# Pairs of heads in a two-layer trunk: bias and x loads behind the weights, two modulation chunks into the output projection, one bias tile a pair

## The chip, the core and the metric

One core of a Trainium2 chip runs the whole kernel. The metric is the device time of one execution in microseconds (us), as the median of three runs. Beside it stands one execution taken by the profiler, from which all durations below come. TensorE (PE) multiplies; VectorE (DVE), ScalarE (ACT) and GpSimd (POOL) work on tiles; all loads of weights, biases and modulation chunks are issued by SyncE (SP), in the order of its queue.

## The reference

A trunk of two layers on x of 256 tokens by 1024 features, in float32. Layer 0 mixes tokens by dilated sliding-window attention, layer 1 by gated linear attention; a gated ConvFFN follows each. Each sub-layer's input is normalised and shifted, scaled and gated by terms worked out from a conditioning vector c. The change lies in layer 0's attention:

```python
qkv = (h @ w_in).reshape(B, S, A_GROUPS, 3, A_HEADS, A_HEAD_DIM)   # 3 dilations, 16 heads of 64
for g, (window, dilation) in enumerate(A_CONFIGS):
    o, lse = dilated_branch(q[g] * scale, k[g], v[g], rel_bias[g], window, dilation)
...
s = einsum(qb, kk) + bias          # bias depends on the distance and the head alone
p = exp(s - max(s)); o = p @ vv / sum(p)
...
o = sum(softmax(lse over g) * o_g) @ w_out
```

## The kernel before

**Products.** Every float32 product is made of three on TensorE: with a weight split into a high part `whi` and a remainder `wlo`, and the input into `hhi` and `hlo`, `mm3` (L172) adds hi by hi, hi by lo and lo by hi. `split` (L155) loads a weight into a `raw` buffer (L159), ScalarE casts it to `whi` in two halves (L165), VectorE subtracts to get `wlo` in two halves (L169). There are four `raw` buffers and three pairs of `whi` and `wlo`. A `raw` buffer is free again when its `wlo` is made.

**Modulation.** The terms from c come in 48 chunks of 1 MB. `ada_chunk` (L129) loads one into a `raw` buffer of the same four (L133), VectorE makes two dot products with c (L138, names `ada_raw` and `dot`), ScalarE adds the constants. `next_ada` takes the next chunk of the list; a chunk can be taken anywhere before its terms are wanted.

**Heads in pairs.** The 16 heads go in eight pairs u = 0 to 7. The first stage (0 to 59 us) loads 8 chunks and the weight `w0`, which holds queries and keys of pairs 0 and 1 and the values of pair 0. Then, for the pairs that follow:

- `queries(u, g)` for the three dilations g = 0, 1, 2: weight `wqk` of 1 MB, products into the bank `pqk`, evacuation to `q` (ScalarE) and `k` (VectorE, L492; for g = 0 both parts by L494 to L499), and one `next_ada`;
- `values(u, half)`: two weights `wv` of 768 KB, products into two banks `pv`, one for each half of the tokens. These two banks and those of `pqk` share two buffers of PSUM (tag `p`): a bank can be written again only when its evacuation is done;
- `scores`, `probabilities` (VectorE adds the bias and takes the maximum, ScalarE makes the exponential, VectorE scales), `turn` (transposes `t` on TensorE, copied to `pt` by ScalarE and VectorE in turns), `outputs` (bank `po`, split into `ohi` and `olo`);
- `by_group` copies the two banks `pv` into tiles `v` (L506 to L509), where the tokens stand in order of residue.

`outputs(u - 1)` runs between scores of pair u and its probabilities. After pair 7 comes `project` with the weight `w_out_a`, in which the last pair's transposes and outputs are placed between products.

**Biases.** The bias of a head depends on the distance alone and lies in DRAM as a row (`rows_d`). `load_bias(u)` reads a pair's two rows shifted by partition: for each head and each half of the partitions one load of 64 x 258 (L347) and one of 64 x 2 x 64 (L348), so 8 loads a pair, of 64.5 and 32 KB. `bias_of` places them behind the last weight load that was written.

**Order.** The order on each engine is made by the framework's scheduler from the order in which the code is written and from the hints `behind` and `tc.issue_after`, which put an instruction after another in the scheduler's reckoning. Each engine then runs its list strictly in order. SyncE's DMAs take turns on eight semaphores, so a DMA is issued only when the one eight issues earlier has landed.

The functions and their line numbers in the profile:

Of the kernel before, what the change touches and what calls it, by code (L numbers as in the profile page):

```python
# [11 lines left out]
F32 = mybir.dt.float32  # L12
# [6 lines left out]
P = 128  # L19
D = 1024  # L20
T = 256
# [7 lines left out]
CH = 64  # L29
# [6 lines left out]
NROW = 768  # L36
KEYS = T + 2 * CH
# [20 lines left out]
def trunk(ctx: ExitStack, tc: tile.TileContext, I, out):  # L58
    nc = tc.nc
# [26 lines left out]
    x_all = state.tile([P, KT, T], F32, name="x_all")  # L86
# [158 lines left out]
    @contextmanager  # L245
    def behind(*those):

        with ExitStack() as st:
            for i in those:
                st.enter_context(tc.issue_after(i.ins))  # L250
            yield
# [85 lines left out]
    def load_bias(u):  # L337

        r, both = rows_d[:, :], []
        for hh in range(2):
            b = att.tile([P, KEYS + 2], F32, tag=f"bias{hh}", name="bias")
            at = r.offset + (2 * u + hh) * NROW
            for odd in range(2):
                own = slice(CH * odd, CH * odd + CH)
                nc.sync.dma_start(b[own, 2 * CH :], bass.AP(r.tensor, at + odd, [[4, CH], [1, T + 2]]))  # L347
                nc.sync.dma_start(b[own, 0 : 2 * CH].rearrange("p (g x) -> p g x", g=2),  # L348
                                  bass.AP(r.tensor, at + 512, [[1, CH], [P, 2], [1, CH]]))
            both.append(b[:, :])  # L350
        return both


    sq = wspl.tile([P, 2048], F32, tag="wlo", name="sq").rearrange("p (k t) -> p k t", k=KT)
# [39 lines left out]
        if kt == 1:  # L394
            scale_terms(1)
    with tc.issue_after(last_load[0].ins):
        nc.sync.dma_start(x_all, I["xT"])
        nc.sync.dma_start(rows_d, rows)
        nc.sync.dma_start(small[:, C_CW:], I["small"][:, C_CW:])

# [3 lines left out]
    def next_ada():  # L404
        if rest:
            ada_chunk(*rest.pop(0))
# [94 lines left out]
    def by_group(v, pv, n):  # L501


        copy = (nc.scalar.copy, nc.vector.tensor_copy)[n]
        top, low = slice(0, CH), slice(CH, P)
        copy(v[top, 0 : 2 * P], pv[top, 0 : 2 * P])  # L506
        copy(v[low, :].rearrange("p (g x) -> p g x", g=3)[:, ::2, :], pv[low, 0 : 3 * P].rearrange("p (g x) -> p g x", g=3)[:, ::2, :])
        nc.scalar.copy(v[low, P : 2 * P], pv[top, 2 * P : 3 * P])
        nc.scalar.copy(v[top, 2 * P : 3 * P], pv[low, P : 2 * P])  # L509

    def new_qk():
        q = [[att.tile([P, T], F32R, tag=f"q0{i}", name="q") for i in range(2)]]
# [39 lines left out]
    def bias_of(u):  # L552
        with tc.issue_after(last_load[0].ins):
            return load_bias(u)
# [14 lines left out]
        for i in range(2 * NG):  # L569
            mm3(pqk1[i], parts(w0[kt], 9 * P + P * i), h[kt], s and i % 2 == 0, e and i % 2 == 1)  # L570

    bias = bias_of(0)
    qk0, qk1 = new_qk(), new_qk()
    for g in range(NG):
        evacuate(*qk0, g, pqk0[2 * g], pqk0[2 * g + 1])
# [1 line left out]
    for g in range(NG):  # L577
        evacuate(*qk1, g, pqk1[2 * g], pqk1[2 * g + 1])
    pv = [bank("pv", "p") for _ in range(2)]
    with behind(values(1, 0, pv)):  # L580
        s, last = scores(*qk0)
    with behind(last):
        values(1, 1, pv)
    v0, v = v, by_groups(pv)
    before = probabilities(s, bias)
    for n in range(2):
        next_ada()

    bias = bias_of(1)
    qk = new_qk()  # L590
    with behind(last):
        end = queries(2, 0, *qk)
    with behind(end[1]):
        turn(range(4), *before)
        s, last = scores(*qk1)
# [2 lines left out]
    before = probabilities(s, bias)  # L598

    for u in range(2, NPAIR):  # L600
        bias = bias_of(u)
        if u > 2:
            qk = new_qk()
            with behind(last):
                queries(u, 0, *qk)
        middle, end = queries(u, 1, *qk)
        with behind(middle):
            turn((0, 1), *before)
        with behind(end):
            turn((2, 3), *before)  # L610
        queries(u, 2, *qk)
        pv = [bank("pv", "p") for _ in range(2)]
        end = values(u, 0, pv)
        if u < NPAIR - 1:
            end = values(u, 1, pv)
        with behind(end):
            s, last = scores(*qk)
        with behind(last):
            last = outputs(u - 1, v, before[1])
        if u == NPAIR - 1:  # L620
            with behind(last):
                values(u, 1, pv)
        v = by_groups(pv)
        before = probabilities(s, bias)
# [9 lines left out]
    def project(src, o_of, l, sub, between=None):  # L634

        ends = []
        shift_columns(l, 1)

        def tile_of(n):
            ps = [bank("py", ("sppt" if between else "ppst")[n])] * 2  # L640
            if n == 3:
                ps[1] = bank("py", "s")
            return split(src[n], 2048), ps

        def products(n, w, ps, order):
            for kt, i in order:
                with behind(*(ends[n - 2 :][:1] if (n, kt) == (2, 2) else ())):
                    e = mm3(ps[i][:, T * i : T * i + T], parts(w, 2 * P * kt + P * i), o_of(kt),
                            kt == 0 and (n == 3 or i == 0), kt == KT - 1 and (n == 3 or i == 1))
                if between and i == 1 and n < 2:  # L650
                    with behind(e):
                        between(n, kt)
            return e

        def leave(n, ps):
            for i in range(2):
                residual(l, sub, 2 * n + i, ps[i][:, T * i : T * i + T])
                add_square(2 * n + i)
                scale(l, 1, 2 * n + i)

        order = [(kt, i) for kt in range(KT) for i in range(2)]
        first = []
        if between:
            first = [tile_of(n) for n in range(2)]
            for n in range(2):
                products(n, *first[n], order[:-2])
        for n in range(4):
            w, ps = first[n] if n < len(first) else tile_of(n)
            if n == 3:
                order.sort(key=lambda x: x[1])  # L670
            ends.append(products(n, w, ps, order[-2:] if n < len(first) else order))
            if n == 3:
                early = load_early(I["w_up"][l, 0])
            leave(n, ps)
        return early

    early = project(I["w_out_a"], lambda kt: (o_hi[kt], o_lo[kt]), 0, 0, between)
# [489 lines left out]
```

## Time and profile before

| | us |
|---|---|
| time, median of 3 runs (782.33 to 782.85) | 782.69 |
| the profiled execution | 783.19 |
| its span, first to last instruction | 781.4 |
| PE busy | 760.2 |
| DVE busy | 640.4 |
| ACT busy | 479.4 |
| POOL busy | 12.4 |

The span begins with the first instruction and ends with the last; 1.8 us of the profiled execution lie outside it. The mean granted clock of TensorE is 0.988 of full speed. The attention of layer 0 takes the span up to about 262 us, the output projection of layer 0 the stretch to about 294 us. An idle time in square brackets behind an instruction is that of its engine just before it, with what released it.

### The profile page before, as it was taken

The page shows a single profiled execution, that of the slowest core. Times are in us where ns is not written, and L with a number is a line of the kernel's source. Part 1 is how long each engine was busy: PE and PEld are TensorE (multiplying, and loading weights), DVE is VectorE, ACT ScalarE, POOL GpSimd, SP SyncE. Part 2 cuts the span into 40 slices and gives each one's busy share as a digit, 9 for nine tenths or more (in the row PEclk, how much of TensorE's full clock was granted, in tenths as well). Part 3 has the DMA queues.
Part 4 walks back from the last instruction along what each step waited for, and adds up shares of the span by engine and source line. Part 5 has one row for each costly group of instructions (what it writes and reads, how often), then busy time and mean ns, then how long its engine had stood idle before and what let it go on. Part 6 is the DMA issues. An engine that isn't in the chain of part 4 may idle for free.

```text
span 781.4 us, 15909 instructions
## 1 busy us (share of the span) xinstructions
PE 760.2 (97%) x6416; PEld 734.3 (94%) x6416; DVE 640.4 (82%) x1152; ACT 479.4 (61%) x932; POOL 12.4 (2%) x36
## 2 busy tenths in 40 slices
PE   8997989999999999999999999999999999999997
PEld 5996979999999999999999998898999999999996
DVE  6997688788789958999998877797668898899662
ACT  5565455555646657866666656655667866667552
POOL 0000000000000010000000100000010000000000
PEclk9998999999999999999999999999999999999999
DMA  9988685776877746777745993966345665555651
GB/s 348 418 327 311 224 286 167 306 271 242 315 248 277 273 135 244 252 258 244 253 143 196 342 336 135 363 231 230 133 144 183 241 216 174 205 189 210 224 187 55
DMA packets 36200, 186.30 MB, mean 238 GB/s; under 512 B 8412, under 2 KB 10972, under 8 KB 19870
## 3 DMA queue, kind: packets, MB, share of 16 engines
q1 hardware_dynamic: 35744, 184.84, 66.0%
q8 instruction: 50, 0.82, 0.4%
q10 hardware_dynamic: 382, 0.45, 0.2%
q14 instruction: 24, 0.20, 0.1%
HBM read 184.17 MB, written 1.10 MB: 237 GB/s over the span
## 4 chain that ended last, share of the span: by engine, by line
PE 67%; DMA 15%; DVE 13%; ACT 3%; issue 1%; SPq 0%; ACTq 0%; DVEq 0%
PE pab L175 10%; PE pab L176 10%; PE pab L177 10%; DMA raw<-in_wqk 7%; DVE wlo L169 7%; PE pd L175 5%; PE pd L176 5%; PE pd L177 5%; DMA raw<-in_wv 4%; DVE ada_raw L138 3%; PE py L177 2%; PE py L176 2%; PE py L175 2%; ACT whi L165 2%; DMA bias<-rows_d 1%
## 5 line engine op out<-in xcount | busy, mean ns | idle before, releaser
L169 DVE TENSOR_TENSOR wlo<-raw,whi 128x1024 fp32r<-128x1024 f32 (+3 forms) x274 | 291.8, 1098 | 50.5 <-ACT whi L165 49.7
L165 ACT CAST whi<-raw 128x1024 fp32r<-128x1024 f32 (+3 forms) x274 | 245.6, 944 | 116.2 <-PE pab L176 41.3
L177 PE MATMUL pab<-hhi,wlo 128*128 128x256 f32 x672 | 184.9, 276 | 0.0
L176 PE MATMUL pab<-hlo,whi 128*128 128x256 f32 x672 | 184.8, 277 | 0.0
L175 PE MATMUL pab<-hhi,whi 128*128 128x256 f32 x672 | 183.4, 277 | 0.0
L175 PE MATMUL pqk<-hhi,whi 128*128 128x256 f32 x440 | 122.2, 289 | 7.1 <-ACT whi L165 4.2
L177 PEld LDWEIGHTS pab<-hhi,wlo 128*128 128x128 f32 x672 | 126.2, 188 | 0.0
L176 PEld LDWEIGHTS pab<-hlo,whi 128*128 128x128 f32 x672 | 126.0, 188 | 0.2
L175 PEld LDWEIGHTS pab<-hhi,whi 128*128 128x128 f32 x672 | 125.2, 188 | 0.1
L177 PE MATMUL pqk<-hhi,wlo 128*128 128x256 f32 x440 | 122.8, 284 | 1.0 <-DVE wlo L169 1.0
L176 PE MATMUL pqk<-hlo,whi 128*128 128x256 f32 x440 | 122.9, 283 | 0.0
L138 DVE CUSTOM_DVE_ANT_0 ada_raw<-ada_raw,c_bc 128x1024 f32<-128x1024 f32 x96 | 113.6, 1222 | 10.7 <-DMA ada_raw<-in_w_ada 10.7
L176 PE MATMUL pd<-glo,whi 128*128 128x256 f32 x352 | 97.1, 276 | 0.0
L177 PE MATMUL pd<-ghi,wlo 128*128 128x256 f32 x352 | 97.1, 276 | 0.0
L175 PE MATMUL pd<-ghi,whi 128*128 128x256 f32 x352 | 96.8, 276 | 0.0
L175 PEld LDWEIGHTS pqk<-hhi,whi 128*128 128x128 f32 x440 | 83.7, 195 | 8.6 <-ACT whi L165 4.5
L177 PEld LDWEIGHTS pqk<-hhi,wlo 128*128 128x128 f32 x440 | 84.2, 192 | 1.7 <-DVE wlo L169 1.3
L176 PEld LDWEIGHTS pqk<-hlo,whi 128*128 128x128 f32 x440 | 84.4, 192 | 0.1
L176 PEld LDWEIGHTS pd<-glo,whi 128*128 128x128 f32 x352 | 66.1, 188 | 0.0
L177 PEld LDWEIGHTS pd<-ghi,wlo 128*128 128x128 f32 x352 | 66.1, 188 | 0.0
L175 PEld LDWEIGHTS pd<-ghi,whi 128*128 128x128 f32 x352 | 65.9, 188 | 0.0
L728 ACT ACTIVATE r<-pab,small 128x256 f32<-128x256 f32 x86 | 46.7, 558 | 15.5 <-DVE r L731 15.4
(214 smaller groups left out, 1267.3 us busy)
## 6 DMA issues: line engine op xcount, KB each, us to landing
ada_raw<-in_w_ada SPq DMA_DIRECT2D x47, 1024.0 KB, 6.3
raw<-in_w_up SPq DMA_DIRECT2D x42, 1024.0 KB, 4.9
raw<-in_w_down SPq DMA_DIRECT2D x32, 704.0 KB, 5.5
raw<-in_wqk SPq DMA_DIRECT2D x18, 1024.0 KB, 7.8
raw<-in_wv SPq DMA_DIRECT2D x14, 768.0 KB, 4.4
raw<-in_w SPq DMA_DIRECT2D x7, 960.0 KB, 6.4
raw<-in_w_out_a SPq DMA_DIRECT2D x4, 1024.0 KB, 7.3
raw<-in_w_v_b SPq DMA_DIRECT2D x4, 1024.0 KB, 6.1
```

The costliest lines, as they stand in the source:

```text
L138: nc.vector.tensor_tensor_reduce(w, w, c_bc, op0=ALU.mult, op1=ALU.add, scale=1.0, scalar=0.0, accum_out=dot,)
L165: copied[0] = nc.scalar.copy(hi[:, c], raw[:, c])
L169: last_lo[0] = nc.vector.tensor_tensor(lo[:, c], raw[:, c], hi[:, c].bitcast(F32), op=ALU.subtract)
L175: mm(ps, a[0], b[0], start=start, stop=False)
L176: mm(ps, a[0], b[1], start=False, stop=False)
L177: return mm(ps, a[1], b[0], start=False, stop=stop)
L728: nc.scalar.activation(r, u[:, :T], AF.Identity, scale=cw[2], bias=col(C_CB + 44 * l + f))
```

## The change

It has five parts.

1. `load_bias` makes one tile [128, 2, 386] a pair instead of two tiles, with 6 loads instead of 8: two of 64 x 2 x 258 and four of 64 x 2 x 64.
2. The load of x in its original layout (`x_all` from `xT`, 1 MB) moves from ahead of the attention to behind pair 2's second weight.
3. The biases of pair 0 are loaded behind the first values weight of pair 1, those of pair 1 behind the first queries weight of pair 2, those of a later pair behind its second queries weight; before, each stood ahead of these.
4. Two chunks move: the two `next_ada` after pair 0's probabilities are gone, and `project` takes one after each of its first two tiles.
5. In `by_group`, which copies the values' banks, the second bank's copy of the low partitions goes from VectorE to ScalarE, and the small copy of the top partitions from ScalarE to VectorE.

```diff
@@ load_bias
-        r, both = rows_d[:, :], []
-        for hh in range(2):
-            b = att.tile([P, KEYS + 2], F32, tag=f"bias{hh}", name="bias")
-            at = r.offset + (2 * u + hh) * NROW
-            for odd in range(2):
...
-                nc.sync.dma_start(b[own, 2 * CH :], bass.AP(r.tensor, at + odd, [[4, CH], [1, T + 2]]))
...
+        b = att.tile([P, 2, KEYS + 2], F32, tag="bias", name="bias")
+        at = r.offset + 2 * u * NROW
+        for odd in range(2):
+            own = slice(CH * odd, CH * odd + CH)
+            nc.sync.dma_start(b[own, :, 2 * CH :], bass.AP(r.tensor, at + odd, [[4, CH], [NROW, 2], [1, T + 2]]))
+            for hh in range(2):
+                nc.sync.dma_start(b[own, hh, 0 : 2 * CH].rearrange("p (g x) -> p g x", g=2),
+                                  bass.AP(r.tensor, at + NROW * hh + 512, [[1, CH], [P, 2], [1, CH]]))
@@ behind the first stage
-        nc.sync.dma_start(x_all, I["xT"])
@@ by_group
         copy(v[top, 0 : 2 * P], pv[top, 0 : 2 * P])
-        copy(v[low, :].rearrange(...)[:, ::2, :], pv[low, 0 : 3 * P].rearrange(...)[:, ::2, :])
+        copy(v[top, 2 * P : 3 * P], pv[low, P : 2 * P])
+        nc.scalar.copy(v[low, :].rearrange(...)[:, ::2, :], pv[low, 0 : 3 * P].rearrange(...)[:, ::2, :])
         nc.scalar.copy(v[low, P : 2 * P], pv[top, 2 * P : 3 * P])
-        nc.scalar.copy(v[top, 2 * P : 3 * P], pv[low, P : 2 * P])
@@ pairs 0 and 1
-    bias = bias_of(0)
     qk0, qk1 = new_qk(), new_qk()
...
-    with behind(values(1, 0, pv)):
+    end = values(1, 0, pv)
+    bias = bias_of(0)
+    with behind(end):
         s, last = scores(*qk0)
...
     before = probabilities(s, bias)
-    for n in range(2):
-        next_ada()
-
-    bias = bias_of(1)
+
     qk = new_qk()
     with behind(last):
         end = queries(2, 0, *qk)
+    bias = bias_of(1)
@@ pairs 2 to 7
-        bias = bias_of(u)
...
         middle, end = queries(u, 1, *qk)
+        bias = bias_of(u)
+        if u == 2:
+            with tc.issue_after(last_load[0].ins):
+                nc.sync.dma_start(x_all, I["xT"])
@@ project
             leave(n, ps)
+            if n < len(first):
+                next_ada()
```

The scheduler orders the engines anew. SyncE's queue after the first stage, before (`in_wv` are the values weights of pair 1, `in_wqk` the first queries weight of pair 2):

```order
L159 DMA raw<-in_wv 128x1536 x2
L347 DMA bias<-rows_d 64x258
L348 DMA bias<-rows_d 64x2x64
L347 DMA bias<-rows_d 64x258
L348 DMA bias<-rows_d 64x2x64
L347 DMA bias<-rows_d 64x258
L348 DMA bias<-rows_d 64x2x64
L397 DMA x_all<-in_xT 128x2048
L347 DMA bias<-rows_d 64x258
L348 DMA bias<-rows_d 64x2x64
L133 DMA ada_raw<-in_w_ada 128x2048 x2
```

After these eight more bias loads stand ahead of the first `in_wqk`. Now:

```order
L159 DMA raw<-in_wv 128x1536 x2
L346 DMA bias<-rows_d 64x2x258
L348 DMA bias<-rows_d 64x2x64
L346 DMA bias<-rows_d 64x2x258
L348 DMA bias<-rows_d 64x2x64
L159 DMA raw<-in_wqk 128x2048
L346 DMA bias<-rows_d 64x2x258
L133 DMA ada_raw<-in_w_ada 128x2048
L348 DMA bias<-rows_d 64x2x64
L346 DMA bias<-rows_d 64x2x258
L348 DMA bias<-rows_d 64x2x64 x3
L159 DMA raw<-in_wqk 128x2048
```

The weight of pair 2 has moved ahead of all but four bias loads, and x and both chunks behind it.

ScalarE's list at pairs 0 and 1, before (`v_736` and `v_851` are value copies of pair 0's second and of pair 1's first bank, `whi_933` the cast of pair 2's first weight):

```order
L498 CAST k_709<-pqk_353 128x256
L491 ACTIVATE q_725<-pqk_360 128x256
L508 COPY v_736<-pqk_357 64x128
L509 COPY v_736<-pqk_357 64x128
L498 CAST k_719<-pqk_358 128x256
...
L506 COPY v_851<-pv_753 64x256
L507 COPY v_851<-pv_753 64x2x128
...
L448 ACTIVATE prob_865,m_861<-prob_865,m_861 128x386
L165 CAST whi_933<-raw_931 128x1024 x2
```

Now (`v_725` and `v_847` are those value copies, `whi_899` and `whi_1076` the casts of pair 2's first two weights):

```order
L496 CAST k_698<-pqk_352 128x256
L165 CAST whi_899<-raw_897 128x1024 x2
L489 ACTIVATE q_714<-pqk_359 128x256
L506 COPY v_725<-pqk_356 64x2x128
L507 COPY v_725<-pqk_356 64x128
L496 CAST k_708<-pqk_357 128x256
L165 CAST whi_1076<-raw_1074 128x1024 x2
...
L446 ACTIVATE prob_861,m_857<-prob_861,m_857 128x386
L504 COPY v_847<-pv_742 64x256
L505 COPY v_847<-pv_742 64x128
```

Casts of coming weights now stand ahead of value copies, and the exponentials ahead of pair 1's.

VectorE's list between pairs 6 and 7, before (`k_2655` is pair 6's last key copy, `wlo_2922` the second values weight, `wlo_3063` pair 7's first queries weight, `ada_raw` a chunk):

```order
L169 TENSOR_TENSOR wlo_2922<-raw_2919,whi_2921 128x768 x2
L465 COPY pt_2635<-t_2811 128x384
L492 COPY k_2655<-pqk_2824 128x256
L138 ISA ada_raw_2875,dot_2877<-ada_raw_2875,c_bc_97 128x1024
...
L169 TENSOR_TENSOR wlo_3063<-raw_3060,whi_3062 128x1024 x2
L506 COPY v_3001<-pv_2886 64x256
```

Now (`k_2607`, `wlo_2881` and `wlo_3012` are the same three):

```order
L169 TENSOR_TENSOR wlo_2881<-raw_2878,whi_2880 128x768 x2
L463 COPY pt_2597<-t_2770 128x384
L169 TENSOR_TENSOR wlo_3012<-raw_3009,whi_3011 128x1024 x2
L490 COPY k_2607<-pqk_2783 128x256
L138 ISA ada_raw_2834,dot_2836<-ada_raw_2834,c_bc_97 128x1024
...
L169 TENSOR_TENSOR wlo_3083<-raw_3080,whi_3082 128x1024
L504 COPY v_2960<-pv_2845 64x256
```

The key copy and the chunk's dots now follow the low parts of the next pair's weight. SyncE's waits move with it: pair 7's first `in_wqk` waited for the dots of the chunk after pair 6's second projection and now waits for those after its first; its third waited for the low parts of the first and now waits for the dots that follow `k_2607`; the second `in_wv` waited for a chunk's dots and now waits for the low parts of the first `in_wv`.

More of the change, by code (lines that the diff above doesn't have):

```diff
@@ L337, in load_bias @@
     def load_bias(u):
-        r, both = rows_d[:, :], []
-        for hh in range(2):
-            b = att.tile([P, KEYS + 2], F32, tag=f"bias{hh}", name="bias")
-            at = r.offset + (2 * u + hh) * NROW
-            for odd in range(2):
[L346 to L351, printed above, removed]
+        r = rows_d[:, :]
+        b = att.tile([P, 2, KEYS + 2], F32, tag="bias", name="bias")
[6 more added lines that the diff above has]
+                                  bass.AP(r.tensor, at + NROW * hh + 512, [[1, CH], [P, 2], [1, CH]]))
+        return [b[:, hh, :] for hh in range(2)]
     sq = wspl.tile([P, 2048], F32, tag="wlo", name="sq").rearrange("p (k t) -> p k t", k=KT)
@@ L506, in by_group @@
         copy(v[top, 0 : 2 * P], pv[top, 0 : 2 * P])
-        copy(v[low, :].rearrange("p (g x) -> p g x", g=3)[:, ::2, :], pv[low, 0 : 3 * P].rearrange("p (g x) -> p g x", g=3)[:, ::2, :])
+        copy(v[top, 2 * P : 3 * P], pv[low, P : 2 * P])
+        nc.scalar.copy(v[low, :].rearrange("p (g x) -> p g x", g=3)[:, ::2, :], pv[low, 0 : 3 * P].rearrange("p (g x) -> p g x", g=3)[:, ::2, :])
         nc.scalar.copy(v[low, P : 2 * P], pv[top, 2 * P : 3 * P])
-        nc.scalar.copy(v[top, 2 * P : 3 * P], pv[low, P : 2 * P])
     def new_qk():
```

## The prediction

> **What bounds the kernel now.** I read the page first: the time of each engine and the clock by slices.
>
> ```profile
> PE 760.2 (97%) x6416; PEld 734.3 (94%) x6416; DVE 640.4 (82%) x1152; ACT 479.4 (61%) x932; POOL 12.4 (2%) x36
> PEclk9998999999999999999999999999999999999999
> ```
>
> TensorE works 97% of the span, so a change that adds or removes no products can only win what TensorE waits or runs at a lower clock. The change touches 44 to 294 us; between 60 and 270 us these are the longest waits of TensorE (us in total, times, longest):
>
> ```profile
> PE pqk L175 <- ACT whi L165: 4.2, 1, 4.2
> PE po L471 <- ACT v L509: 2.7, 1, 2.7
> PE pqk L177 <- DVE wlo L169: 1.0, 1, 1.0
> ```
>
> Two places, then. Next the stretches around them (columns: from and to, length, busy time and count of PE, PEld, DVE, ACT, POOL, then granted clock, DMA share, GB/s), with three clean ones for comparison: the end of pair 2's first projection, pair 0's outputs, and a whole later pair; the last two rows serve the sums below.
>
> ```profile
> 69.68:73.88 4.20, 0.00 (x1) 0.00 (x0) 3.51 (x16) 4.17 (x13) 0.00 (x0) 0.83 1.02 423
> 75.64:79.22 3.58, 3.58 (x16) 3.58 (x17) 2.46 (x3) 1.99 (x2) 0.00 (x0) 0.50 1.03 384
> 79.22:82.74 3.52, 3.52 (x31) 3.52 (x31) 0.98 (x1) 0.00 (x0) 0.00 (x0) 0.99 0.61 117
> 111.81:114.54 2.73, 0.00 (x1) 0.03 (x1) 2.68 (x5) 1.44 (x3) 0.00 (x0) 0.79 0.72 300
> 114.54:117.30 2.76, 2.76 (x25) 2.00 (x25) 2.76 (x8) 0.00 (x0) 0.00 (x0) 0.50 0.38 71
> 93.58:95.06 1.48, 1.48 (x25) 1.12 (x24) 0.84 (x6) 1.05 (x2) 0.00 (x0) 1.00 0.79 237
> 117.30:120.12 2.82, 2.82 (x15) 2.82 (x14) 2.07 (x7) 2.70 (x5) 0.00 (x0) 0.50 0.77 322
> 207.66:237.33 29.67, 29.67 (x277) 28.86 (x273) 26.15 (x54) 17.21 (x37) 0.00 (x0) 1.00 0.78 284
> 225.90:230.06 4.16, 4.16 (x26) 4.16 (x25) 3.74 (x7) 1.79 (x4) 0.00 (x0) 1.00 0.61 181
> 262.00:294.00 32.00, 32.00 (x312) 31.01 (x309) 22.69 (x50) 18.99 (x42) 2.38 (x2) 1.00 0.47 171
> ```
>
> After each wait the products run at clock 0.50 for some microseconds. So the first place costs 4.20 + 0.96 (the wlo wait) + the half clock: 16 products in 3.58 us where 31 took 3.52 (0.1135 each, 1.82 for 16), 1.76 lost. That is 6.9 us. The second costs 2.73 + (2.76 - 1.48) + (2.82 - 15 x 0.1135), 5.1 us. Together 12.0. Elsewhere TensorE is full: pair 6 has 29.67 busy of 29.67 us.
>
> Why is pair 2's first weight late? The SP queue tells (start, us of the issue):
>
> ```profile
> 44.01 2.86 SPq L159 DMA_DIRECT2D raw<-in_wv  x2
> 47.70 0.52 SPq L347 DMA_DIRECT2D bias<-rows_d  x1
> 48.27 0.62 SPq L348 DMA_DIRECT2D bias<-rows_d  x1
> 52.16 0.33 SPq L397 DMA_DIRECT2D x_all<-in_xT  x1
> 53.74 1.07 SPq L133 DMA_DIRECT2D ada_raw<-in_w_ada  x2
> 66.56 0.54 SPq L159 DMA_DIRECT2D raw<-in_wqk  x1
> ```
>
> The two values weights are out at 46.9; then SP issues sixteen bias pieces, x and two modulation chunks, and wqk goes at 66.56, while the products that want it could start at 69.68. And the second place:
>
> ```profile
> 110.74 1.99 ACT L165 CAST whi<-raw 128x1024 fp32r<-128x1024 f32 x2 [1.78 <-DMA raw<-in_wqk]
> 111.81 1.23 DVE L169 TENSOR_TENSOR wlo<-raw,whi 128x1024 fp32r<-128x1024 f32 x1 [2.65 <-ACT whi L165]
> 113.84 0.56 DVE L465 COPY pt<-t 128x384 f32<-128x384 f32 x1
> ```
>
> The view of waits names the value copy, but the pt copy that po needs stood on VectorE behind a wlo, whose cast waited for its load: a late weight again.
>
> **The change part by part.**
>
> *Weights first (bias and x later), -12.0.* In the new order wqk of pair 2 stands behind two value weights and four bias pieces: at about 0.6 us a piece it issues near 50.3 instead of 66.56, sixteen microseconds earlier, against a wait of 4.20 + 0.96. The wait must go. At the second place the order now has pt copies ahead of the wlo that waits for a load, so -5.1 too. Bounds: 0 if the wait only moves (a rival), -12.0 if both go. I take -12.0, since the lead is three times the wait.
>
> The Trainium skill ("TensorE: Matmul & The Clock Gate", "HAM oscillation") asks only that no idle gap exceed about 3.4 us. By it the 2.73 us gap should not have cost the clock, yet the trace shows 0.50 behind it: the measurement decides. By the rule the second place would be worth 2.7, and the sum below would be 2.4 us worse.
>
> *Fewer bias issues; the x load.* Two pieces a pair fewer, 8 x 2 x 0.6 us of SP's time, on a queue that after pair 2 waits for buffers: it counts only inside the loop below. The x load moves behind pair 2's second weight and its first user is the projection after 262 us: nothing, and without the cover of those 200 us at most its own 1 MB landing.
>
> *New short waits of TensorE, +2.6.* ScalarE's order now has casts of the coming weight ahead of evacuations that TensorE needs.
>
> ```profile
> 60.63 0.26 ACT L509 COPY v<-pqk 64x128 f32<-64x128 f32 x1
> 61.54 0.34 PE L175 MATMUL pv<-whi,hhi 128*128 128x384 f32 x1
> 69.20 0.37 ACT L506 COPY v<-pv 64x256 f32<-64x256 f32 x1
> 70.22 0.26 ACT L509 COPY v<-pv 64x128 f32<-64x128 f32 x1
> 202.74 2.00 ACT L165 CAST whi<-raw 128x1024 fp32r<-128x1024 f32 x2 [1.28 <-DMA raw<-in_wqk]
> ```
>
> (i) Pair 1's second token tile of values (61.54) takes the bank that the copies ending at 60.89 release. A cast of 2.00 now stands ahead: 2.00 less the slack 0.65 is 1.35. (ii) pair 2's first query product takes a bank released by four value copies, 1.28 us long (69.20 to 70.48), that cannot begin before the first token tile's products end and now stand behind two casts and four exponentials; hidden in the 4.20 before, about 1.3 now. Bounds each 0 (cast early enough) to 3 (its load lands late). I take 2.6.
>
> *Pairs 2 to 7: a loop through the raw buffers, +2.5.* On VectorE the copy of k of the last projection now stands behind the low parts of the next pair's first weight. That copy releases the bank of the second token tile of values and precedes the chunk dots that free the buffer for wqk number three. In the new order one turn is: first wqk lands, cast and low parts, k copy, dots, third wqk lands, cast and low parts, wv lands, cast and low parts, k, dots, next first wqk. Durations from pair 6 (issues on SP, casts, low parts; then the dots' group and the page's rows of loads, KB and us to landing):
>
> ```profile
> 197.35 0.54 SPq L159 DMA_DIRECT2D raw<-in_wqk  x1
> 206.21 0.33 SPq L159 DMA_DIRECT2D raw<-in_wqk  x1
> 213.83 2.00 ACT L165 CAST whi<-raw 128x1024 fp32r<-128x1024 f32 x2 [0.29 <-DMA raw<-in_wqk]
> 214.92 2.36 DVE L169 TENSOR_TENSOR wlo<-raw,whi 128x1024 fp32r<-128x1024 f32 x2
> 217.31 3.94 SPq L159 DMA_DIRECT2D raw<-in_wv  x2
> 221.60 1.57 ACT L165 CAST whi<-raw 128x768 fp32r<-128x768 f32 x2 [1.26 <-DMA raw<-in_wv]
> L138 DVE CUSTOM_DVE_ANT_0 ada_raw<-ada_raw,c_bc 128x1024 f32<-128x1024 f32 x96 | 113.6, 1222 | 10.7 <-DMA ada_raw<-in_w_ada 10.7
> raw<-in_w_up SPq DMA_DIRECT2D x42, 1024.0 KB, 4.9
> raw<-in_wqk SPq DMA_DIRECT2D x18, 1024.0 KB, 7.8
> ```
>
> First wqk: 202.74 - 197.35 = 5.39. Third: 213.83 - 206.21 = 7.62. Cast and low parts 206.21 - 202.74 = 3.47 and 217.28 - 213.83 = 3.45. wv: 221.60 - 217.31 = 4.29, its cast and low parts about 2.5 (half a cast, then two low parts at three quarters of 1.2). Two dots 2.4 a chunk, twice; a k copy 0.4, twice. Without the two wqk loads that is 3.5 + 3.5 + 4.3 + 2.5 + 4.8 + 0.8 = 19.4, less 0.3 of overlap between chained VectorE rows: 19.1. With both loads at the 4.9 of in_w_up's row, the loop is 28.9 and TensorE (29.67) never waits; with 5.39 and 7.62 it is 32.1 and each of five turns waits 2.4. I take 11.1 for the two (5.4 as measured; 5.7 for the third, which issued in before just after a chunk and wqk two, and has only a chunk ahead now): 30.2, 0.5 a turn, +2.5. Ends 0 and +12.
>
> The Trainium skill ("DMA: Bandwidth & Descriptors", "Anatomy of one DMA") fits 2.0 us plus bytes at 436 GB/s, an estimate of 4.4 us for these loads; the rows show 4.9 to 7.6 under traffic. By the fit the term would be 0, and the sum 2.5 better.
>
> *The last pair, +1.0.* There k stands behind w_out's first low parts and fewer products cover it, 12 of the 24 that took 4.16 us (225.90), 2.1. A cast half, two low parts and the copy are 3.7: 1.6 if the load is just in time, 0 if early. I take 1.0.
>
> *Two chunks in the projection, +0.6.* Four dots, 4.9 us of VectorE, enter a stage where VectorE is busy 22.69 of 32 us and TensorE all of it: room for them. They leave pair 0, where VectorE was not the limit. But they stand ahead of the last pair's probabilities, and the last pair's outputs move to just ahead of the products that read them:
>
> ```profile
> 280.20 0.38 ACT L480 CAST ohi<-po 128x256 fp32r<-128x256 f32 x1 [4.30 <-PE po L475]
> 280.61 0.42 DVE L481 TENSOR_TENSOR olo<-po,ohi 128x256 fp32r<-128x256 f32 x1 [4.31 <-ACT ohi L480]
> ```
>
> ohi and olo together are 0.8 us, uncovered but for a product or two: +0.6. Ends 0 and 3 (probabilities late by most of the dots).
>
> *by_group's copies:* one bigger copy from VectorE to ScalarE, a few tenths either way on engines with slack; nothing, and 0.3 a pair if ScalarE's copies release a bank last.
>
> Sum: -12.0 + 2.6 + 2.5 + 1.0 + 0.6 = -5.3. The profiled execution took 783.19 us (span 781.4), 0.5 over the median 782.69: 777.9 by its own time, 777.4 against the median.
>
> **The rivals.**
>
> R1, TensorE stays full: loads as fast as in_w_up's, so the last three terms are nothing. -12.0 + 2.6: 773.3. For it: the pair-6 row is full now. Against it: DMA share 0.78 there, casts waiting for their loads.
>
> R2, the clock goes too: the new waits of 1.3 us, with the loop's, take the clock to 0.50 for some 3 us. One place costs 1.1 to 1.8 (as above), two 2.2 to 3.6: 779 to 781. Against it: the 0.96 wait lies at clock 0.50 already and tells nothing, and the 2.73 gap is twice as long.
>
> R3, the other side: the loop becomes the bound. Place: the k copy behind the next pair's low parts; price: at 7.62 for the third wqk, 32.1 against 29.67, 2.4 x 5 = 12.2. The sum is then -7.8 + 12.2 = +4.4: 787.1. It decides from 7.8 / 5 = 1.56 a turn, loads of 12.1 together. For it: the third load's measured 7.62 and wqk's median of 7.8 on the page. Against it: those stood behind two other loads.
>
> R4, the change doesn't do what it says: wqk goes early but its buffer is not free, or the hole only moves to pair 3: about 782.
>
> **How the numbers follow.** Forecast 0.42, R1 0.22, R2 0.12, R3 0.16, R4 0.08. 0.2% (1.6 us) is about what a measurement of this kernel can tell from no change. Faster: the first three but for a remainder, 0.75; same: R4 and the edge of R3, 0.09; slower: the rest of R3, 0.16. The range 772 to 784 holds R1, R2, R4 and the mild end of R3; the forecast's own is 775.5 to 780.
>
> **What the profile after would show.** TensorE's waits: no 4.2 and no 2.7, clock 1.00 from 60 to 120 us; short waits of pv and pqk on v copies near 62 and 72; pv on k (VectorE) in each pair, 0.5 the forecast, 2.4 R3; pairs of 30.2 us. The prediction is wrong if pairs 3 to 7 take over 31.2 us, or if a wait above 2 us stands anywhere before 120 us.

## The result, and the profile after

| | before | after |
|---|---|---|
| time, median (us) | 781.93 (780.74 to 782.85, 6 runs) | 793.25 (792.26 to 796.82, 6 runs) |
| span of the profiled execution | 781.4 | 791.7 |
| PE busy | 760.2 | 759.7 |

The ratio is 1.0152 (95% interval 1.013 to 1.0173): slower by 1.5%. The forecast was 777.4, in a range of 772 to 784; what came is nearest its rival R3, which the prediction priced at 787.1, and lies 6 us beyond it.

The page of the kernel after, in the lines that answer to those of before: TensorE has the same work in a longer span, and the clock digit falls once.

```profile
PE 759.7 (96%) x6416; PEld 733.6 (93%) x6416; DVE 638.1 (81%) x1152; ACT 480.2 (61%) x932; POOL 12.5 (2%) x36
PEclk9999999899999999999999999999999999999999
```

TensorE's waits between 60 and 270 us (us in total, times, longest). The waits of 4.2 and 2.7 are gone; four waits of a query product and three of a value product on key copies have come.

```profile
PE pqk L175 <- DVE k L497: 9.7, 4, 3.3
PE pv L175 <- DVE k L490: 5.7, 3, 4.7
PE pqk L175 <- ACT v L507: 1.5, 1, 1.5
PE pv L175 <- ACT v L507: 1.2, 1, 1.2
```

The timeline of TensorE from one pair's outputs to the next gives a turn of a pair. The outputs of pair 1 start at 105.53 after against 114.54 before: 9.0 us won. Those of pair 6 start at 271.29 against 262.47: 8.8 lost. Here are the windows from outputs to outputs, pairs 1 to 6, after (columns as in the prediction: length; busy time and count of PE, PEld, DVE, ACT, POOL; clock, DMA share, GB/s):

```profile
105.53:137.53 32.00, 29.75 (x278) 28.41 (x273) 24.13 (x50) 17.09 (x38) 0.20 (x2) 1.00 0.73 257
137.53:173.10 35.57, 32.24 (x278) 31.22 (x273) 26.62 (x55) 18.14 (x42) 0.20 (x2) 0.90 0.71 236
173.10:207.29 34.19, 31.21 (x278) 30.02 (x272) 25.73 (x52) 18.00 (x42) 0.20 (x2) 0.95 0.71 244
207.29:239.62 32.33, 30.05 (x278) 28.52 (x272) 25.41 (x52) 16.92 (x38) 0.00 (x0) 1.00 0.74 256
239.62:271.29 31.67, 26.98 (x256) 25.68 (x249) 25.79 (x53) 14.70 (x32) 0.00 (x0) 0.95 0.74 266
```

TensorE's full turn is 29.67. The first four rows exceed it by 2.3, 5.9, 4.5 and 2.7, in all 15.4 us; in the second and third TensorE is idle for 3.33 and 2.98 us at one place and then works at half clock for a while, which is why its busy time grows too. The fifth, the last pair, was 26.62 before: 5.1 more.

What takes the time shows in the view of the chain that ended last, over the pairs, 137 to 240 us. First before, then after:

```profile
by line: DMA raw<-in_wqk 35.0%; DVE wlo L169 19.7%; DMA raw<-in_wv 14.9%; DVE ada_raw L138 6.6%; ACT whi L165 6.6%; ACT prob L448 3.9%; DVE prob L439 3.7%; issue 2.5%; DVE pn L455 1.8%; DVE pn L454 1.5%; DVE k L499 1.1%; DVE q L495 1.0%; AC
```

```profile
by line: DMA raw<-in_wqk 23.0%; DMA bias<-rows_d 21.0%; DVE wlo L169 15.0%; DMA raw<-in_wv 12.2%; DVE ada_raw L138 10.9%; ACT whi L165 5.5%; issue 5.4%; SPq L348 4.1%; SPq L346 1.7%; DVE pt L463 1.4%; DVE k L497 1.2%; SPq L159 1.0%; DVE k L
```

TensorE is in neither list: followed back from the last instruction of the stretch, the chain runs through loads and splits in both. Before, TensorE was full all the same (29.67 of 29.67 us a turn), so there these loads and splits kept up with it; after, TensorE waits for them. And the loads of the bias, which were not in it, are now a fifth of it. The timeline of one turn (pair 5) shows the loop; SP's queue first, then ScalarE and VectorE:

```profile
172.00 0.54 SPq L159 DMA_DIRECT2D raw<-in_wqk  x1
182.06 7.19 SPq L159 DMA_DIRECT2D raw<-in_wv  x2
191.55 0.33 SPq L159 DMA_DIRECT2D raw<-in_wqk  x1
196.37 0.33 SPq L159 DMA_DIRECT2D raw<-in_wqk  x1
198.03 0.61 SPq L346 DMA_DIRECT2D bias<-rows_d  x1
204.37 1.38 SPq L348 DMA_DIRECT2D bias<-rows_d  x2
205.85 0.54 SPq L159 DMA_DIRECT2D raw<-in_wqk  x1
```

```profile
178.59 2.00 ACT L165 CAST whi<-raw 128x1024 fp32r<-128x1024 f32 x2 [5.16 <-DMA raw<-in_wqk]
186.21 1.56 ACT L165 CAST whi<-raw 128x768 fp32r<-128x768 f32 x2 [2.67 <-DMA raw<-in_wv]
188.82 0.42 DVE L497 TENSOR_TENSOR k<-pqk,k 128x256 fp32r<-128x256 f32 x1
197.56 2.00 ACT L165 CAST whi<-raw 128x1024 fp32r<-128x1024 f32 x2 [1.67 <-DMA raw<-in_wqk]
200.92 0.41 DVE L490 COPY k<-pqk 128x256 f32<-128x256 f32 x1
```

From third weight to third weight is 205.85 - 172.00 = 33.85. In it are the third wqk's load, 178.59 - 172.00 = 6.59, the first wqk's load, 197.56 - 191.55 = 6.01, and a new piece. The chunk's dots behind the key copy at 200.92 end at 203.5, and the third wqk could go; but SP stands at the last two bias pieces, issued at 204.37 and 205.18, which wait for the bias loads issued at 196.75 and 198.03 to land (204.35 and 205.11). That hold is 2.3 us. The rest, 33.85 - 6.59 - 6.01 - 2.3 = 18.95, is what the prediction summed to 19.1. The chain that ended last leaves this path for the later one, by the second wqk's issue and the bias load:

```profile
196.37 0.33 SPq L159
198.03 7.08 DMA bias<-rows_d
205.85 5.60 DMA raw<-in_wqk
```

Why the pieces wait: the program has a wait between them and the earlier load. SP's waits of the kernel after, 107 to 262 us (us in total, times, longest):

```profile
SPq L348 <- DMA bias<-rows_d: 13.8, 5, 4.3
```

The eight semaphores are not the reason: the DMA eight issues ahead of the piece at 204.37 is the wqk of 191.55, which had landed when its cast began at 197.56. In the new tile the load of 64 x 2 x 258 spans both heads, and the second head's small piece lies between its two parts. The two write different columns, but the span of the one covers the other, which is the likely reason for the wait. The traces bear it out as far as they go: each late piece is let go by the landing of the wide load of its own half, and the wait stands in every run with one tile and the bias loads on SP's queue (after, e2, e3, e6, e9, e12, e13) and in none with two tiles. A tile in which no piece lies within another's span was not tried with six loads. The load that is waited for also takes longer in this place, in the view of DMA issues from 137 to 235 us (KB each, us to landing), first after and then before:

```profile
bias<-rows_d SPq DMA_DIRECT2D x6, 129.0 KB, 7.1
```

```profile
bias<-rows_d SPq DMA_DIRECT2D x12, 64.5 KB, 3.1
```

### The profile page after: what moved, and what is told of

The parts are those of the page before. It is cut to its first block, busy times and chain, and to the rows that moved or that the text cites. A ratio compares the mean times of both kernels' runs of the same rounds, so it can differ in the third digit from the quotient of the medians.

```text
span 791.7 us, 15903 instructions
## 1 busy us (share of the span) xinstructions
PE 759.7 (96%) x6416; PEld 733.6 (93%) x6416; DVE 638.1 (81%) x1152; ACT 480.2 (61%) x932; POOL 12.5 (2%) x36
## 4 chain that ended last, share of the span: by engine, by line
PE 68%; DMA 13%; DVE 13%; ACT 3%; issue 2%; SPq 1%; ACTq 0%; DVEq 0%
PE pab L175 10%; PE pab L176 10%; PE pab L177 10%; DVE wlo L169 6%; PE pd L175 5%; PE pd L176 5%; PE pd L177 5%; DMA raw<-in_wqk 5%; DVE ada_raw L138 4%; DMA bias<-rows_d 4%; DMA raw<-in_wv 2%; PE py L176 2%; PE py L175 2%; PE py L177 2%; ACT whi L165 2%
## 5 line engine op out<-in xcount | busy, mean ns | idle before, releaser
L138 DVE CUSTOM_DVE_ANT_0 ada_raw<-ada_raw,c_bc 128x1024 f32<-128x1024 f32 x96 | 113.2, 1218 | 11.1 <-DMA ada_raw<-in_w_ada 11.1
L175 PE MATMUL pv<-whi,hhi 128*128 128x384 f32 (+1 forms) x144 | 50.0, 359 | 6.9 <-DVE k L490 5.7
```

Source lines behind the costliest of these rows:

```text
L138: nc.vector.tensor_tensor_reduce(w, w, c_bc, op0=ALU.mult, op1=ALU.add, scale=1.0, scalar=0.0, accum_out=dot,)
L175: mm(ps, a[0], b[0], start=start, stop=False)
```

## The experiments

All times are compared with the kernel before on the same chip (medians of 782.1 us for e1 to e4, 783.1 for e5 to e8, 781.8 for e9 to e11 and 782.0 for e12 to e14). Where two runs are held against each other, it is by what each wins or loses against its own kernel before.

**e1: bias loads on another queue.** Edit, in the kernel after:

```diff
-            nc.sync.dma_start(b[own, :, 2 * CH :], ...)
+            nc.gpsimd.dma_start(b[own, :, 2 * CH :], ...)
             for hh in range(2):
-                nc.sync.dma_start(b[own, hh, 0 : 2 * CH]...)
+                nc.gpsimd.dma_start(b[own, hh, 0 : 2 * CH]...)
```

> The changed kernel with its six bias loads a pair issued by GpSimd's queue instead of SP's; the VectorE order of pairs 2 to 7 stays that of the changed kernel (k copy behind the next pair's low parts). Loop theory: one turn (third wqk issue to third wqk issue, 33.85 us in pair 5) loses only the 2.3 us that SP stood at the bias pieces, 31.5, still 1.9 over TensorE's 29.6: about 783 (780 to 786), waits of pqk on k and of pv on k remain at 1 to 2 us each pair. Rival 1, the SP hold alone is the cause: turns of 29.6 to 30, 772 to 776, no wait of TensorE over 1 us after 105 us. Rival 2, the copies and chunks (parts 4 and 5) are the cause: unchanged at 793.

Measured: 783.31, ratio 1.0017 (0.9993 to 1.004). The loop theory's number was met: the turns from outputs to outputs are 31.15, 31.00, 31.46 and 30.38, and waits on the key copies remain, up to 1.0 us in these turns and 2.8 in the last pair.

```profile
PE pv L175 <- DVE k L490: 5.4, 5, 2.8
PE pqk L175 <- DVE k L497: 2.2, 3, 0.9
```

So the bias loads on SP's queue are 10 us of the loss (1.2 lost here, 11.3 in the kernel after). At 2.3 us a turn most of that is the hold; the edit also takes the pieces' issue time and their turns on the eight semaphores off SP, which was not told apart.

**e2: key copies ahead.** Edit, in the kernel after: `low` and `late` hints on two splits.

```diff
-        w = split(I["wqk"][u - 2, g], 2048)
+        first = (keyed[u - 1, 2],) if (u - 1, 2) in keyed and g == 0 else ()
+        w = split(I["wqk"][u - 2, g], 2048, low=first, late=first)
...
-            w = split(I["wv"][u - 1, half], 1536)
+            first = (keyed[u, 0],) if u > 1 else ()
+            w = split(I["wv"][u - 1, half], 1536, low=first, late=first)
```

> The changed kernel with two hints: the low parts of a pair's first queries weight come behind the key copy of the pair before, and those of its first values weight behind the first projection's key part. SP's queue keeps its bias pieces between the second and third queries weight. Loop theory: the k copies no longer wait for a load, turns fall to 29.6 to 30.2, about 776 (772 to 780), no wait of TensorE on k above 1 us. Rival 1, the SP hold alone: the third weight stays late, 788 to 793. Rival 2 (parts 4 and 5): 793.

Measured: 796.13, ratio 1.0178 (1.0143 to 1.0213). The loop theory missed by 20 us. The hints did put the key copies first, but the scheduler moved the third weight's low parts behind the probabilities' scaling, and SP's hold stayed. So moving the key copies is not enough; what their place costs by itself this run does not tell.

**e3: one bias tile alone.** Edit: the kernel before with part 1.

> The kernel before with part 1 alone (one bias tile a pair, six loads); biases stay ahead of the weights. The scheduler gives it the VectorE order of the changed kernel in pairs 2 to 7 (k copy behind the next pair's low parts). Loop theory: the two early gaps stay (12 us) and pairs 2 to 7 lose 1 to 4 us each: 788 to 798. Rival 1, the hold between the second and third weight alone, which is not there: 781 to 783. Rival 2 (parts 4 and 5, not there): 781 to 783.

Measured: 794.18, ratio 1.0164 (1.0119 to 1.021), in the loop theory's range. Part 1 alone, with the bias loads still ahead of the weights, makes the kernel slower: the scheduler takes the new order, and five value products wait on key copies. But a hold is here too, against what was expected: SP's bias pieces wait 8.8 us in five waits for bias loads to land (8.3 in e6). So neither e3 nor e6 tells the order from the hold.

```profile
PE pv L175 <- DVE k L491: 13.6, 5, 3.7
```

**e4: the first pairs alone.** Edit: the kernel before with part 2, and part 3 for pairs 0 and 1 only.

> The kernel before with only the first pairs changed: biases of pairs 0 and 1 and the x load behind the weights; bias tiles, later biases, chunks and copies as before. VectorE's order in pairs 3 to 7 is that of the kernel before. Loop theory: the early gaps go (-12, less new waits of 1 to 3) and the pairs keep 29.6 to 30: 771 to 775. Rivals 1 and 2 say the same; if it does not come under 778, the early term itself was wrong.

Measured: 774.17, ratio 0.9907 (0.9883 to 0.9931). The early term was right: the waits of 4.2 and 2.7 go, and turns stay at 29.64 to 30.13. This kernel beats both others: 7.9 us under the kernel before.

```profile
137.03:166.67 29.64, 29.47 (x277) 28.47 (x272) 25.23 (x51) 17.84 (x40) 0.20 (x2) 1.00 0.74 264
166.67:196.80 30.13, 29.69 (x279) 28.64 (x273) 25.66 (x53) 17.38 (x39) 0.20 (x2) 1.00 0.76 274
```

**e5: all but the bias parts.** Edit: e4 with parts 4 and 5.

> The kernel of e4 (first pairs alone) with parts 4 and 5 added: the two chunks in the projection and the other copies of values; bias tiles and the biases of later pairs as in the kernel before. On VectorE the key copies stand ahead of the next pair's low parts, as before. Loop theory: 772 to 777, no turn over 30. Rival 2 (chunks and copies carry the loss): 783 or more.

Measured: 779.82, ratio 0.9967 (0.9948 to 0.9985): three microseconds over the range. The turns are 29.41, 30.41, 31.51 and 29.95, two of them over the 30 that was forecast; 4.22 us stand at 75.19, where pair 2's first product waits for the value copies.

**e6: e4 and one tile.** Edit: e4 with part 1.

> The kernel of e4 with part 1 added (one tile, six loads a pair), biases of later pairs ahead of the weights. The scheduler now puts the key copy behind the next pair's low parts. Loop theory: turns of 31 to 32.5, 782 to 788, pv and pqk wait on k each pair. Rival 1 (only the hold between second and third weight costs): 773 to 777, since four of the six bias loads now stand ahead of the first queries weight and two behind it.

Measured: 796.94, ratio 1.0171 (1.0144 to 1.0197). Against e4 part 1 costs 21.8 us (13.8 lost where e4 won 7.9). Right in sign, but 9 us over the loop theory's range: the turns are 35.22, 31.29, 33.58 and 33.70, and as in e5 4.25 us stand early.

**e7: e4 and the later pairs' biases behind the second weight.** Edit: e4 with the whole of part 3, in two tiles.

> The kernel of e4 with the later pairs' biases behind the second queries weight, in the two tiles and eight loads of the kernel before. On VectorE the key copy keeps its place ahead of the next pair's low parts; SP's third queries weight comes behind eight bias issues that wait for earlier loads through the eight semaphores. If the order on VectorE alone makes the loop: 773 to 778. If the hold on SP costs by itself, as e2 suggests: 780 to 790, with the third queries weight issued 7 us or more after the second.

Measured: 793.61, ratio 1.013 (1.0113 to 1.0148). With the tiles of before and the key copies first it loses nearly as much as e6: 18.4 us against e4, and 3.6 over the range given for a hold. SP's waits between 107 and 262 us tell what holds the third weight (us in total, times, longest): bias pieces wait for the queries weights eight issues ahead to land, and the third weight behind them.

```profile
SPq L347 <- DMA raw<-in_wqk: 14.1, 5, 3.4
```

**e8: e1 and e2 together.** Edit: the hints of e2, the bias loads on GpSimd's queue.

> Both hints of e2 and the bias loads on GpSimd's queue as in e1: neither cause is left. Loop theory in its two halves (hold and order): 771 to 776, turns of 29.6 to 30. If e2's loss was a new loop through the probabilities and not the hold: 780 or more.

Measured: 791.57, ratio 1.0102 (1.0062 to 1.0142). Missed. The hints cost 7.3 us against e1. Chain of waits, 137 to 236 us:

```profile
by line: DMA raw<-in_wqk 51.8%; DVE wlo L169 14.7%; ACT whi L165 12.8%; DVE ada_raw L138 7.2%; DVE pn L452 4.7%; issue 3.2%; DVE pn L453 2.4%; PE pv L175 2.4%; PE pv L177 1.9%; PE pv L176 1.8%; DVE k L497 1.3%; ACT k L496 1.2%; DVE olo L479
```

Half the chain is now queries loads: the order that the hints made runs through the probabilities, the key part, the chunk's dots and the values weight before the next queries load may go.

**e9 and e10: a buffer of their own for the chunks**, in the kernel after and in e4:

```diff
-        raw = wraw.tile([P, 2048], F32, tag="raw", name="ada_raw")
+        raw = att.tile([P, 2048], F32, tag="ada", name="ada_raw", bufs=1)   # in the attention
```

> The changed kernel, with the chunks of the attention and projection loaded into a buffer of their own in the attention's pool, so that the four raw buffers serve the weights alone. Order on VectorE as in the changed kernel (key copy behind the next pair's low parts), bias pieces still between the second and third queries weight. Loop theory (chunks and weights free each other's buffers in a circle): a weight now waits only for the low parts four weights earlier, turns fall from 32 to 35 to 29.6 to 30.5, 773 to 780. If the order on VectorE or SP's hold costs by itself, whatever the buffers: 785 or more.

> The kernel of e4 with the same buffer of its own for the chunks. Loop theory: e4's turns were at TensorE's 29.6 already, so only its short waits can go: 770 to 775. The scheduler moves the key copy behind the next pair's low parts and the biases behind the second weight here too; if that order costs by itself: 780 or more.

Measured: 797.05 (1.0194, 1.0163 to 1.0224) and 802.34 (1.0255, 1.0224 to 1.0287). Both missed, and they settle nothing on the four buffers: one buffer makes a loop of its own, in which a chunk's load waits for the dots of the one before. SP's longest wait in e9, 137 to 262 us:

```profile
SPq L134 <- DVE dot L139: 30.4, 12, 3.2
```

**e11: e4 and the chunks in the projection.** Edit: e4 with part 4.

> The kernel of e4 with part 4 alone added (two chunks into the projection). It tells whose the 5.6 us between e4 and e5 are. If the chunks (first queries product waits 4.2 us on the value copies, which stand behind the cast of the second queries weight): 778 to 781. If the copies of part 5: 773 to 775.

Measured: 779.88, ratio 0.9973 (0.995 to 0.9995): what lies between e4 and e5 (4.6 us) is part 4's, which costs 6.1 here. Some of it is early: the cast of the second queries weight stands ahead of the value copies on ScalarE, and pair 2's first product waits 2.8 us for them, against 0.9 in e4; the clock is 0.50 behind this wait and 1.00 behind that of e4.

**e12: each queries weight in two loads.** Edit, in the kernel after:

```diff
-        w = split(I["wqk"][u - 2, g], 2048)
+        w = split(I["wqk"][u - 2, g], 2048, 2)
```

> The changed kernel with each queries weight loaded by two DMAs of 512 KB, so that the cast and low part of the first half begin while the second half is still coming; the orders on VectorE and SP are otherwise those of the changed kernel. Loop theory (a turn of 33.85 us in pair 5 holds two queries loads, their casts and low parts): about 1.2 us less at each of the two, turns of 31 to 32, 783 to 788. If the turn is not set by these loads but by SP's hold at the bias pieces alone: 791 to 795.

Measured: 800.0, ratio 1.0228 (1.0203 to 1.0253). Missed, in the wrong direction: SP's wait of bias pieces for bias landings between 107 and 262 us grew from 13.8 to 17.5 us. Three more DMAs a pair go through the same eight semaphores, which is a likely cause but was not tried by itself.

**e13: no chunks in the pairs.** Edit, in the kernel after:

```diff
         with behind(evacuate(q, k, g, pq, pk)):
-            next_ada()
+            if rest:
+                l, n = rest.pop(0)
+                for s in range(2):
+                    mod[(l,) + ADA_ORDER[2 * n + s]] = mod[0, 0, s]
```

> The changed kernel without the 17 chunks taken in the pairs' queries: no load, no dots, the terms they give are replaced by the first two shift terms. SP's hold at the bias pieces and VectorE's order (key copy behind the next pair's low parts) stay. It also takes 2.4 us of VectorE and 1 MB of loads from each projection. Loop theory: without the dots between key copy and load, and with the weights alone in the four buffers, turns are TensorE's 29.4 to 29.8: 769 to 775. If the order on VectorE or the hold alone costs: turns of 31 or more, 780 or more.

This kernel leaves out the terms of 17 chunks. The four turns from outputs to outputs, pairs 1 to 5 (first and last of four rows):

```profile
107.84:137.70 29.86, 29.86 (x279) 29.05 (x273) 18.77 (x40) 15.84 (x32) 0.20 (x2) 1.00 0.53 173
...
197.43:227.29 29.86, 29.86 (x277) 29.05 (x272) 18.77 (x40) 15.85 (x32) 0.00 (x0) 1.00 0.54 172
```

TensorE is full, 29.86 of 29.86, although the key copies stand behind the next pair's low parts and SP still waits for bias landings there (137 to 262 us):

```profile
SPq L348 <- DMA bias<-rows_d: 8.1, 3, 3.0
```

In these turns neither the order nor the hold costs anything once chunks are out of the loop. Part of that may be less traffic: the DMA share is 0.53 against 0.71 to 0.74. It does not hold for the last pair, which takes 33.66 against 26.62 before. There the key copy stands behind w_out's low parts and the dots of a chunk of the projection, and TensorE waits for it:

```profile
254.58 0.69 PE L175 MATMUL pv<-whi,hhi 128*128 128x384 f32 x1 [5.12 <-DVE k L490]
```

The kernel as a whole took 796.85 (1.0192, 1.0169 to 1.0215), for a reason behind the pairs: between 300 and 420 us TensorE makes 1021 products against 1056 before, at clock 1.00 and with no wait. It was not tested why; the tiles of the missing terms shift the place of those behind them. So only the pairs are read from this run.

**e14: e4 and the two loads of e12.**

> The kernel of e4 with the two half loads of e12. Loop theory: e4's turns are TensorE's already, so only its short waits (0.9, 0.8, 1.2, 0.5 us) can go: 771 to 775, the same as e4 within a measurement.

Measured: 786.02, ratio 1.0057 (1.0036 to 1.0077). Missed by 11 us: turns of 31.0 to 31.5 in place of 29.6. SP's waits for wqk landings between 107 and 262 us doubled, from 12.8 to 24.7 us. In the good order too the two half loads cost time.

## Why the prediction was wrong, by its own steps

**Weights first, -12.0: right.** e4 shows it alone. In the kernel after, pair 1's outputs start 9.0 us earlier, and the half clock behind the second gap (1.3 and 1.1) is spared after that: 11.4 in all, net of new waits of 2.7. So the step itself won about 14 where 12.0 was summed. The same count for e4 gives 12.9: outputs at 106.03, 8.5 us earlier, the same 2.4, and 2.0 of waits ahead of them. What the rest is stays open.

**New waits near 62 and 72 us, 1.35 and 1.3: right.**

```profile
62.67 0.45 PE L175 MATMUL pv<-whi,hhi 128*128 128x384 f32 x1 [1.24 <-ACT v L507]
72.40 0.39 PE L175 MATMUL pqk<-hhi,whi 128*128 128x256 f32 x1 [1.46 <-ACT v L507]
```

**The loop, +2.5: this step failed.** The four turns lost 15.4 us; at 32.0 to 35.6 they are past the 31.2 that the prediction named as its sign of being wrong. Its mechanism, the k copies behind a split and the chunk's dots behind them, was there, and its fixed part too (18.95 against 19.1). Three things were mis-sized or left out. The two loads together took 12.6 where I took 11.1, near my upper end of 13.0 (5.39 and 7.62). SP's hold of 2.3 a turn was left out altogether: the step said of the bias pieces that they count only inside the loop, and then did not count them; they stand ahead of the third weight in SP's queue, and the landing they wait for took 7.1 us there. And in the two worst turns TensorE waited long enough to lose its clock, 2.6 and 1.5 us on top of the waits of 3.33 and 2.98; the turns of 32.00 and 32.33 kept it. The Trainium skill ("DMA: Bandwidth & Descriptors", "Anatomy of one DMA") gives the fit that the prediction set beside these loads for DMAs issued by GpSimd; these are SP's, so for this term only the measured loads count. The place was another than I named: TensorE waited mostly at the third projection, for the first projection's key part (L497), which stands behind the values weight's low parts, and only three times at the value products.

**The last pair, +1.0: 5.1.** The key copy waited for w_out's load, its cast and its low parts, as said, but the load was not just in time. It was not issued late: 15.7 us behind pair 5's outputs (255.34 - 239.62), against 17.5 before (253.34 - 235.85, where pair 5's outputs start there). It took 6.9 us to land, and the product that wanted the bank could have started at 261.45.

```profile
255.34 2.95 SPq L159 DMA_DIRECT2D raw<-in_w_out_a  x2
263.39 2.36 DVE L169 TENSOR_TENSOR wlo<-raw,whi 128x1024 fp32r<-128x1024 f32 x2 [2.26 <-ACT whi L165]
265.67 0.42 DVE L490 COPY k<-pqk 128x256 f32<-128x256 f32 x1
```

TensorE's wait there is 4.69, where the step gave 1.6 for a load just in time. With faster turns it stays: 2.8 in e1, and 5.1 in e13, where a chunk's dots stand ahead of the key copy too.

```profile
266.14 0.69 PE L175 MATMUL pv<-whi,hhi 128*128 128x384 f32 x1 [4.69 <-DVE k L490]
```

**The chunks in the projection, +0.6: 1.5.** The wait on ohi is 0.5 us, as summed. From pair 6's outputs to the end of the projection the same 302 products take 1.5 us longer, first before and then after; beside that wait they follow each other more slowly at clock 1.00, and why stays open.

```profile
262.47:297.50 35.03, 35.03 (x302) 33.46 (x297) 24.60 (x53) 20.95 (x47) 2.38 (x2) 1.00 0.47 164
271.29:307.80 36.51, 36.03 (x302) 34.31 (x297) 25.87 (x56) 22.61 (x51) 2.41 (x2) 1.00 0.48 168
```

And e11 shows that the move costs 6.1 against e4, a part of it early, where the order on ScalarE changes without them: the step looked for its cost in the projection alone.

**by_group, nothing: right** as far as e5 and e11 tell, which differ in it alone (779.82 and 779.88, or 3.3 and 1.9 under their own kernel before). **R3** was the case nearest to what came, priced 787: it had the loads' upper end, but not the hold, the clock nor the wait for w_out. **R2** did not come at the places it named, where waits of 1.24 and 1.46 kept the clock at 1.00; but the clock fell in the two longest new waits between 140 and 200 us and in the last pair's.

**The sum.** Against the kernel before, the profiled execution is 9.0 us ahead at pair 1's outputs; the next four turns lose 12.8 (the half clock that they had before is in this), the last pair 5.1, and what follows 1.4. That is 10.3, the difference of the spans, 791.7 and 781.4.

The cause, as far as it is shown: the four turns are held by a loop through loads, splits and chunk dots. The bias loads on SP's queue, with the hold at their last pieces, are 10 us of the loss (e1); without chunks in the loop these turns lose nothing (e13). What stays open is how much of the 9 us by which e1 lies behind e4 is the order on VectorE, since every edit that moved it (e2, e8) made the scheduler move other things as well and every run with one tile on SP's queue has the hold, and how much of e13's relief is its lighter traffic.

## What to carry to other kernels

Before a change of an order is priced by the waits it removes, close the loop of buffers in the new order: which load waits for which release, what stands ahead of that release on its engine and ahead of the load on the issuing queue, and whether one turn stays under the busy engine's own, with each load at its measured upper value. A tile merged from two can cost more than the issues it saves, if its strided load covers another piece's columns and a wait follows between them. Test the parts apart: here two of the five, for the first pairs alone, won 0.9%, either of the other two bias edits turned that into a loss (e6, e7), and the moved chunks took most of it back (e11).

## What the runs showed of the hardware that was not expected

The granted clock behind a wait of TensorE, kernel after: behind a wait of 1.80 us it stays 1.00, behind 3.33, 2.98 and 4.69 it falls (windows from the first product behind each wait):

```profile
222.40:226.00 3.60, 3.60 (x31) 3.60 (x32) 3.60 (x8) 1.23 (x4) 0.00 (x0) 1.00 0.84 255
154.16:158.00 3.84, 3.84 (x18) 3.84 (x19) 3.84 (x8) 1.50 (x5) 0.00 (x0) 0.50 0.82 245
189.38:193.00 3.62, 3.62 (x22) 3.62 (x22) 3.62 (x8) 1.50 (x5) 0.00 (x0) 0.67 0.79 249
266.14:269.00 2.86, 2.86 (x9) 2.86 (x10) 2.86 (x5) 0.29 (x1) 0.00 (x0) 0.50 0.90 275
```

The other runs show that there is no sharp edge. First e3 behind a wait of 3.04 us, then e7 behind one of 1.91:

```profile
268.92:272.00 3.08, 3.08 (x24) 2.82 (x24) 2.23 (x4) 0.93 (x2) 0.00 (x0) 1.00 0.86 279
154.62:158.00 3.38, 3.38 (x17) 3.38 (x18) 3.38 (x6) 1.70 (x5) 0.00 (x0) 0.56 0.65 229
```

In all sixteen traces, 44 to 300 us, waits up to 1.85 us left the clock at 1.00 (but for the 0.96 of the kernel before, which lies in a stretch at half clock already), and those of 3.13 and more lost it. Of the 22 between, 13 lost it and 9 kept it, in no order of length. A stretch at half clock there lasts 3.4 us or two or three times that (kernel after: 190.58 to 194.00 and 153.04 to 159.87; e9: 266.25 to 276.49). So a wait of this length can cost up to 1.7 us of clock, or up to 3.4, or nothing; whether the half clocks that the prediction counted come in every execution is not shown. A rule of the Trainium skill ("TensorE: Matmul & The Clock Gate", "HAM oscillation") puts the edge above about 3.4; 1.91 in e7, and 2.73 and 2.98 in the kernels before and after, lie below that and lost the clock, so the measurement decides.

And the landing of a small load depends much on its place: the bias loads of 129 KB took 7.1 us in SP's queue between the weights; in the same queue behind the values weights they took 5.0 (e3) and 5.2 (e6), and in GpSimd's queue, in e1, from 137 to 235 us:

```profile
bias<-rows_d POOLq DMA_DIRECT2D x6, 129.0 KB, 3.6
```
